# Sixteen pairs of modulation vectors of a hybrid layer, computed between the heads of the mixer instead of in the first feed-forward half

## The chip, the cores and the metric

The kernel runs on one core of a Trainium2 chip. The metric is the device time of one execution in microseconds, as the median of several runs. The engines are named as in the profile: PE is TensorE's matmuls, PEld its weight loads, DVE is VectorE, ACT is ScalarE, POOL is GpSimd, SP is the engine whose queue issues nearly all transfers of this kernel. A wait that an engine's next instruction meets stops everything behind it in that engine's queue.

## The reference

One layer of a diffusion backbone on 512 latent and 256 context tokens of 1024 features, in float32. Nine modulation vectors of 1024 features come from one matrix product on the conditioning vector (`c` for the latents, `c_ctx` for the context), and scale, shift or gate the three sub-layers:

```
mx = silu(c) @ w_ada + b_ada          # split into nine vectors, mx[0] .. mx[8]; mc the same from c_ctx
x = x + 0.5 * mx[2] * swiglu(modulate(rmsnorm(x, norm1_w), mx[0], mx[1]), ffn1_w_in, ffn1_w_out)
u = modulate(rmsnorm(x, norm2_w), mx[3], mx[4])
p = u @ w_mix_in                      # q, k, v of 8 heads, decays, gates, pooling input, branch gates
x = x + mx[5] * mixer(p)              # 8 heads of a two-way delta-rule scan, a pooling branch, output projection
x = x + 0.5 * mx[8] * swiglu(modulate(rmsnorm(x, norm3_w), mx[6], mx[7]), ffn2_w_in, ffn2_w_out)
out = rmsnorm(x, final_norm_w)
```

The context goes through the first two lines and through the mixer's q, k, v with its own vectors. Vectors 0 to 4 are needed before the mixer begins; 5 is needed only after the last head, at the mixer's output, and 6 to 8 only in the second feed-forward half.

## The kernel before

All big products take float32 operands as two parts of a shorter format, so each becomes three matmuls (`whi` by `hhi`, `whi` by `hlo`, `wlo` by `hhi`); a weight tile is loaded into a staging tile and split by a cast on ACT (`whi`, L119) and a subtraction on DVE or POOL (`wlo`, L120). The order of the instructions on each engine is made by a scheduler when the program is built, from the order of the code and its own idea of when things are ready; on the chip each engine then follows its fixed order.

The 72 feature tiles of the nine modulation vectors are computed in pairs by `ada_steps`. A pair takes two loads of 512 KB of `w_ada` into the staging tile `stg`, of which there are two and which all weights of `weights` share; 16 matmuls of a 32-column operand `sc` (L150); a copy of the sums to `ada` on DVE (L153); two transposes on PE (L157); a reduction (L159) and two additions of the bias (L162) on DVE. `ada_steps` is a generator that stops once, after the copy.

- The first sixteen tiles of vectors 0 and 1 are made ahead of the first half-step, from a staging pool of their own.
- Tiles 16 to 71, which are 28 pairs, are in the list `ada_left`. The first half-step (`ffn`) calls `trickle` four times in each group's output projection and twice in each pair of its input projection. Each call finishes the pair that is open and starts the next one, so a pair's copy lies a whole call away from its transposes. 26 pairs go this way. `LATE = 2` pairs are left, which are computed whole, by `ada`, after the half-step's call.
- The mixer then runs ten iterations of a loop over k. In one, the scan of head k (`scan`), the inverses of head k+1 (`invert`) and the norms of head k+2 (`front`) are interleaved by the string `ORDER`; then come the projections of head k+3 (`head`: weights of k, q and v, products at L132, a short convolution L583), the gate of head k+1 (`gate`) and some of the 16 branch gates (`extra`, by the table `SHARE`, which has 3 and 2 in the first two iterations, 6 and 5 in the last two and none between). The products of L132 need no scan and stand between the scan's short matmuls in PE's order. The scan's first matmul in an iteration is L973 with `vt` on its left.

The SP queue issues the loads of `stg` (L110 for weights, L146 for `w_ada`), of the decay rows `crow` (L808), and the stores of each head's result `y` (L1017) and of the branch gates (L1033), in one fixed order; a load of `stg` waits until the tile's last reader is done.

Of the kernel before, what the change touches and what calls it, by code (L numbers as in the profile page):

```python
# [41 lines left out]
def layer_kernel(ctx, tc, a, out):  # L42
# [42 lines left out]
    sc = xs.tile([128, KT, 32], F32, name="sc")  # L85
# [21 lines left out]
    def weights(src, k0, nk, c0, engs=(act, dve)):  # L107
        """128 columns of a matrix, in two float32r parts."""
# [5 lines left out]
    def halves(w, first=act, second=dve):  # L114
        """Up to four feature tiles of 128 columns, in two float32r parts."""
# [7 lines left out]
    def job(w, act_hi, act_lo, ks, parts, new=None):  # L123
        """One tile of 128 output features: w (K on the partition) times the activations."""
# [16 lines left out]
    def ada_steps(cts, tags="bb", room=None):  # L141
# [10 lines left out]
        s = xs.tile([128, 256], F32, tag="ada", name="ada", bufs=1)  # L152
# [5 lines left out]
        r = xs.tile([128, 2, 2], F32, tag="adar", name="adar", bufs=2)  # L158
# [6 lines left out]
    def mod_scale(n, k, mod, rn):  # L165
        """(1 + scale) * norm weight for feature tile k."""
        dve.tensor_scalar(out=eff[:, n, k, :], in0=mods[:, mod * 8 + k, :], scalar1=1.0,
                          scalar2=vec[:, 0, rn + k:rn + k + 1], op0=ALU.add, op1=ALU.mult)
# [5 lines left out]
    def rstd_of(ssq, n, dim):  # L174
        """ssq: [128, n] sums of squares with the token on the partition."""
# [23 lines left out]
    def rstd_rows(tmp, acc, parts, ssq=None, tag="b", dtag=("diag", 1)):  # L199
        """Root mean square, inverted, of every token, the same on all partitions."""  # L200
# [29 lines left out]
    # [C11 C12; C21 C22] = [A11 A12; A21 A22] [B11 B12; B21 B22], rows: two tiles of 128 output features,  # L230
    # columns: two halves of the tokens, inner: two halves of the 8 feature tiles
    def products(n2, more):
        """The places of the right-hand operands: B11, B21, B22, T4, T1, T2, T3, and B12."""
# [9 lines left out]
    def blocks_of(t, k, n2, dst):  # L243
        """The blocks of B themselves, of feature tile k."""
# [3 lines left out]
    def blocks(dst):  # L248
        """The operands of the products of the blocks themselves."""
        return lambda j, part, k: dst[(0, 7)[j] if k < 4 else (1, 2)[j]][part][:, k % 4]  # L250

    def combine(tmp, b11, b12, b21, b22, n2, put, bufs=1, eng=dve):
        """The other right-hand operands from the blocks; overwrites b12, and without bufs b11 and b22."""
# [19 lines left out]
    def side_by_side(ws, outs, rhs, ks):  # L273
        """Products of several weights, one feature tile k of all of them after another."""
# [7 lines left out]
    def plain(src, c0, rhs, n2, k0=0, nk=KT, tags=None):  # L282
        """As quad, by eight multiplications, from the blocks themselves."""
# [8 lines left out]
    def quad_weights(tmp, deep, src, c0, rows=None):  # L292
        """256 columns of src on their way to the seven left-hand operands, in the order of their use."""
# [3 lines left out]
        for i in range(2):  # L297
            # the inner halves: the first and the last four feature tiles, or the even and the odd ones
# [21 lines left out]
    class Quads:  # L320
        """The quads of a list of (src, c0, rows), one after another."""
# [15 lines left out]
    def quad(quads, gen, w1, w6, rhs, n2):  # L337
        """Two tiles of output features of all tokens: C11 (in PSUM), C12, C21, C22."""
# [155 lines left out]
    def last_pair(ahi, alo):  # L494
        """The last two feature tiles' share of the output, first for the latents, and the mixer's input from it."""
# [7 lines left out]
        w_first.extend(weights(a["w_mix_in"], 0, KT, c) for c in (3 * D, D))  # L503
        for k in range(KT):
            mod_scale(2, k, 4, R_N2)
# [23 lines left out]
    LATE = 2  # L529
    ada_left = [(t, t + 1) for t in range(16, 72, 2)]  # L530
# [3 lines left out]
    def trickle():  # L534
        for g in ada_open:
            next(g, None)
            if len(ada_left) == 24:
                mod_gate(1, 2, True)
# [8 lines left out]
    while ada_left:  # L547
        ada(ada_left.pop(0), "ag")
    mod_gate(3, 5, False)
# [39 lines left out]
    def head(h):  # L589
        """Project, convolve k, q and v of one head."""  # L590
# [640 lines left out]
```

## Time and profile before

| | |
|---|---|
| median of 3 runs | 1804.71 us |
| lowest and highest | 1804.62 and 1808.05 us |
| span of the profiled execution | 1807.2 us |
| PE busy | 1649.1 us (91%) |
| PEld busy | 1486.5 us (82%) |
| DVE busy | 1365.7 us (76%) |
| ACT busy | 943.9 us (52%) |
| POOL busy | 632.3 us (35%) |
| moved by DMA | 184.06 MB, 102 GB/s on the mean |

The span is that of one execution taken by the profiler; it lies inside the range of the timed runs and 2.5 us above their median. The first half-step's products run from about 84 to 600 us of it, the mixer's input from there to about 640 us, the scans of the eight heads from about 740 to 1236 us, and the rest is the mixer's output and the second half-step. Busy shares are a mean over all of these, so a stage is read by its own stretch.

### The profile page before, as it was taken

To read this page: it belongs to the slowest core of one execution; us is meant where nothing else is said; L and a number is where in the kernel's file an instruction comes from. 1 tells how busy PE (TensorE), PEld (TensorE's weight loads), DVE (VectorE), ACT (ScalarE), POOL (GpSimd) and SP (SyncE) were. 2 spreads that over 40 slices of the span, in tenths; PEclk is the share of its full clock that TensorE was granted. 3 is DMA by queue.
4 is the path that set the end of the run, shared out by engine and by line. 5 is a ranking of instruction groups with operands and counts; after the bars stand their busy time and mean duration, and the time that the engine had idled before them with its cause. 6 is when DMAs were issued, how large, how long until landed. Compare 5 with 4: busy or idle time off the path is not lost.

```text
span 1807.2 us, 34927 instructions
## 1 busy us (share of the span) xinstructions
PE 1649.1 (91%) x13432; PEld 1486.5 (82%) x13432; DVE 1365.7 (76%) x2647; ACT 943.9 (52%) x2088; POOL 632.3 (35%) x669
## 2 busy tenths in 40 slices
PE   6899999999999999899999999999987888888886
PEld 4798998989999778777877888777877888888886
DVE  5778888897878874457776778645549899899886
ACT  5533343434344465757777776564426444444454
POOL 2244434444534020332233321100005556555642
PEclk9999999999999999999999999999998999899988
DMA  9455455351212353522221212247431222222221
GB/s 272 117 147 160 133 144 156 110 161 62 76 59 71 117 169 120 130 64 60 53 59 47 67 40 66 59 132 224 129 105 48 77 88 83 82 82 85 79 82 59
DMA packets 250971, 184.06 MB, mean 102 GB/s; under 512 B 7008, under 2 KB 238133, under 8 KB 250677
## 3 DMA queue, kind: packets, MB, share of 16 engines
q1 hardware_dynamic: 250368, 181.65, 34.4%
q8 instruction: 106, 1.74, 0.4%
q14 instruction: 60, 0.49, 0.1%
q10 hardware_dynamic: 437, 0.18, 0.0%
HBM read 170.22 MB, written 11.58 MB: 101 GB/s over the span
## 4 chain that ended last, share of the span: by engine, by line
PE 55%; DVE 25%; issue 6%; ACT 5%; DMA 5%; POOL 2%; SPq 0%; POOLq 0%; ACTq 0%; DVEq 0%
PE b L132 12%; PE b L345 11%; PE g L345 7%; PE a L345 6%; DVE wlo L120 4%; DVE cv L583 2%; DVE q L474 2%; DVE alo L189 2%; PE b L279 2%; DVE t L257 2%; DVE xT L437 1%; PE a L708 1%; PE a L132 1%; PE b L150 1%; PE g L132 1%
## 5 line engine op out<-in xcount | busy, mean ns | idle before, releaser
L119 ACT CAST whi<-qst 128x512 fp32r<-128x512 f32 (+2 forms) x288 | 159.1, 554 | 164.7 <-PE b L345 66.7
L120 DVE TENSOR_TENSOR wlo<-qst,whi 128x512 fp32r<-128x512 f32 (+2 forms) x288 | 215.5, 757 | 16.7 <-ACT whi L119 16.4
L119 ACT CAST whi<-qs 128x512 fp32r<-128x512 f32 (+2 forms) x216 | 117.7, 554 | 171.4 <-POOL qs L309 82.1
L132 PE MATMUL b<-hhi,whi 128*128 128x512 f32 (+1 forms) x528 | 188.4, 386 | 0.0
L132 PE MATMUL b<-hlo,whi 128*128 128x512 f32 (+1 forms) x528 | 188.3, 385 | 0.0
L132 PE MATMUL b<-hhi,wlo 128*128 128x512 f32 (+1 forms) x528 | 187.7, 386 | 0.0
L308 POOL TENSOR_TENSOR qs<-qst 128x512 f32<-128x512 f32 (+2 forms) x72 | 92.7, 1287 | 253.1 <-DMA qst<-in_ffn_w_in_dram 70.2
L313 POOL TENSOR_TENSOR qs<-qst,qs 128x512 f32<-128x512 f32 (+2 forms) x72 | 87.4, 1214 | 198.1 <-DVE wlo L120 181.1
L119 ACT CAST whi<-stg 128x512 fp32r<-128x512 f32 x154 | 94.3, 620 | 112.7 <-PE b L132 70.4
L120 DVE TENSOR_TENSOR wlo<-qs,whi 128x512 fp32r<-128x512 f32 (+2 forms) x144 | 104.9, 728 | 49.7 <-ACT whi L119 49.4
L345 PE MATMUL b<-ehi,wlo 128*128 128x384 f32 (+1 forms) x240 | 84.3, 351 | 45.7 <-DVE wlo L120 45.7
L179 POOL TENSOR_TENSOR rs<-rs,mhalf 128x4 f32<-128x4 f32 (+2 forms) x13 | 14.0, 1077 | 294.6 <-DVE rs L177 279.0
L188 ACT CAST ahi<-q 128x384 fp32r<-128x384 f32 (+1 forms) x118 | 55.3, 473 | 118.1 <-DVE q L474 60.8
L583 DVE SCALAR_TENSOR_TENSOR cv<-raw,vec,cv 128x772 f32<-128x772 f32 (+1 forms) x96 | 100.4, 1046 | 11.6 <-ACT cv L581 8.3
L345 PE MATMUL g<-hhi,whi 128*128 128x384 f32 (+1 forms) x320 | 105.5, 330 | 2.5 <-ACT whi L119 2.5
L345 PE MATMUL g<-hhi,wlo 128*128 128x384 f32 (+1 forms) x320 | 103.6, 324 | 3.6 <-DVE wlo L120 3.6
L132 PEld LDWEIGHTS b<-hlo,whi 128*128 128x128 f32 x528 | 94.6, 191 | 14.9
L132 PEld LDWEIGHTS b<-hhi,whi 128*128 128x128 f32 x528 | 94.5, 191 | 14.9
L132 PEld LDWEIGHTS b<-hhi,wlo 128*128 128x128 f32 x528 | 94.0, 191 | 15.0
L345 PE MATMUL g<-hlo,whi 128*128 128x384 f32 (+1 forms) x320 | 103.6, 324 | 0.0
L120 POOL TENSOR_TENSOR wlo<-stg,whi 128x512 fp32r<-128x512 f32 x46 | 65.4, 1429 | 90.6 <-ACT whi L119 70.5
L312 POOL TENSOR_TENSOR qst<-qst 128x512 f32<-128x512 f32 (+2 forms) x72 | 95.6, 1327 | 0.6
(480 smaller groups left out, 5459.6 us busy)
## 6 DMA issues: line engine op xcount, KB each, us to landing
qst<-in_ffn_w_in_dram SPq DMA_DIRECT2D x80, 512.0 KB, 3.5
stg<-in_w_ada_dram SPq DMA_DIRECT2D x56, 512.0 KB, 4.6
stg<-in_w_mix_in_dram SPq DMA_DIRECT2D x49, 512.0 KB, 3.9
qst<-in_ffn_w_out_dram SPq DMA_DIRECT2D x40, 256.0 KB, 2.7
adx<-in_w_ada_dram SPq DMA_DIRECT2D x16, 512.0 KB, 7.1
qst<-in_ffn_w_out_dram SPq DMA_DIRECT2D x16, 512.0 KB, 3.8
crow<-cumd SPq DMA_DIRECT2D x16, 384.0 KB, 8.8
stg<-in_ffn_w_in_dram SPq DMA_DIRECT2D x8, 512.0 KB
```

The lines of the kernel that those rows point to most:

```text
L119: (first.copy if first is act else first.tensor_copy)(out=hi[:, :n], in_=w)
L120: second.tensor_tensor(out=lo[:, :n], in0=w, in1=hi[:, :n], op=ALU.subtract)
L132: pe.matmul(res[p][:, :m], lhsT=ww(i), rhs=hh(k)[:, o:o + m], start=(i == 0 and j == 0), stop=(i == n - 1 and j == 2))
L188: act.copy(out=hi, in_=src)
L189: dve.tensor_tensor(out=lo, in0=src, in1=hi, op=ALU.subtract)
L257: eng.tensor_tensor(out=t, in0=x, in1=y, op=ALU.subtract)
L279: pe.matmul(x, lhsT=ww(k), rhs=rhs(j, part, k), start=n + e == 0, stop=n + e == len(ks) + 1)
L308: pool.tensor_tensor(out=s1, in0=a21, in1=a22, op=ALU.add)
L312: pool.tensor_tensor(out=a21, in0=a11, in1=a21, op=ALU.subtract)
L313: pool.tensor_tensor(out=s2, in0=a12, in1=s2, op=ALU.subtract)
L345: pe.matmul(o, lhsT=ww[:, k], rhs=rhs(j, part, k), start=first and k + i == 0, stop=k + i == nh + 1, skip_group_check=not first)
L583: dve.scalar_tensor_tensor(out=cv[:, :n], in0=raw[:, t:t + n], scalar=tap[t], in1=cv[:, :n], op0=ALU.mult, op1=ALU.add)
```

## The change

`ada_left` keeps only tiles 16 to 39 (12 pairs: vectors 2, 3 and 4), and `LATE` is 0, so that all of them go through `trickle`. The other 16 pairs (vectors 5 to 8) are in a new list `ada_late`. The mixer's loop takes from it by the table `ADA_SHARE`, after the branch gates of an iteration: two pairs in each of the iterations k = 0 and 1, three in each of k = 2 to 5. There `ada` runs a pair whole, without the stop between the copy and the transposes. The tiles `sc`, `ada` and `adar` move to pools that live longer, and the gate of vector 5 (`mod_gate(3, 5, False)`) follows the loop. Apart from that, comments are gone.

```diff
-    sc = xs.tile([128, KT, 32], F32, name="sc")
+    sc = base.tile([128, KT, 32], F32, name="sc")
...
-        s = xs.tile([128, 256], F32, tag="ada", name="ada", bufs=1)
+        s = wp.tile([128, 256], F32, tag="ada", name="ada", bufs=1)
...
-        r = xs.tile([128, 2, 2], F32, tag="adar", name="adar", bufs=2)
+        r = wp.tile([128, 2, 2], F32, tag="adar", name="adar", bufs=2)
...
         w_first.extend(weights(a["w_mix_in"], 0, KT, c) for c in (3 * D, D))
+        while ada_left or ada_open:
+            trickle()
         for k in range(KT):
...
-    LATE = 2
-    ada_left = [(t, t + 1) for t in range(16, 72, 2)]
+    LATE = 0
+    ada_left = [(t, t + 1) for t in range(16, 40, 2)]
+    ada_late = [(t, t + 1) for t in range(40, 72, 2)]
...
-            if len(ada_left) == 24:
+            if len(ada_left) == len(range(24, 40, 2)):
                 mod_gate(1, 2, True)
...
-    while ada_left:
-        ada(ada_left.pop(0), "ag")
-    mod_gate(3, 5, False)
     fp_cm.__exit__(None, None, None)
...
     SHARE = (3, 2, 0, 0, 0, 0, 0, 0, 6, 5)
+    ADA_SHARE = (0, 0, 2, 2, 3, 3, 3, 3, 0, 0)
...
         for f in extra[:SHARE[k + 2]]:
             f()
+        for cts in ada_late[:ADA_SHARE[k + 2]]:
+            ada(cts)
+        ada_late = ada_late[ADA_SHARE[k + 2]:]
         extra = extra[SHARE[k + 2]:]
-    assert not extra
+    assert not extra and not ada_late
+    mod_gate(3, 5, False)
```

What it does to the order on the engines shows at three places.

On PE, in an output projection of the first half-step (`ahi`, `alo` are the two parts of its right operand), one pair goes; the rows with a minus stood there before:

```order
 L345 MATMUL b<-alo,whi 128x384
 L345 MATMUL b<-ahi,wlo 128x384
-L157 MATMUL b<-ident,ada 128x128 x2
-L150 MATMUL b<-stg,sc 32x128 x16
 L345 MATMUL g<-ahi,whi 128x384
 L345 MATMUL g<-alo,whi 128x384
```

The transposes of one pair and the matmuls of the next stood between two products; now the products follow each other.

On PE, at the start of a head's scan in the mixer, before (`vt`, `kf`, `qf` are the head's v, k and q, `S` the scan's state, `hhi` and `hlo` the input of the projections):

```order
L973 MATMUL g<-vt,L 128x128 x2
L764 MATMUL a<-ident,kf 128x128 x6
L985 MATMUL g<-vw,kt 128x128 x2
L771 MATMUL a<-ident,qf 128x128 x4
L824 MATMUL a<-kf 128x128 x4
L952 MATMUL g<-S,kf 128x128 x2
L132 MATMUL b<-hhi,whi 128x512
L132 MATMUL b<-hhi,whi 128x256
L132 MATMUL b<-hlo,whi 128x512
```

And after the change, further into such a start, from the transposes of the second of three pairs to the first product of the next head's weights; the first pair's matmuls stand ahead of `L973 g<-vt,L`, its transposes between the six of `L764`, and the second pair's matmuls before these rows:

```order
L824 MATMUL a<-kf 128x128 x2
L157 MATMUL b<-ident,ada 128x128 x2
L150 MATMUL b<-stg,sc 32x128 x8
L797 MATMUL a<-ident,vf 128x128 x4
L150 MATMUL b<-stg,sc 32x128 x8
L797 MATMUL a<-ident,vf 128x128 x2
L157 MATMUL b<-ident,ada 128x128 x2
L833 MATMUL a<-qf,kf 128x128 x4
L985 MATMUL g<-vw,kt 128x128 x2
L132 MATMUL b<-hhi,whi 128x512
L132 MATMUL b<-hhi,whi 128x256
L132 MATMUL b<-hlo,whi 128x512
```

Before, the products of L132 begin ahead of the second of the scan's steps; now the first of them stands behind the second `L985`, and all three pairs stand ahead of it.

On the SP queue, around the store of one head's result, before:

```order
L1017 DMA yg_dram<-y 128x512
L110 DMA stg<-in_w_mix_in_dram 128x8x128 x2
L808 DMA crow<-cumd 128x6x128
L110 DMA stg<-in_w_mix_in_dram 128x8x128
L808 DMA crow<-cumd 128x6x128
L110 DMA stg<-in_w_mix_in_dram 128x8x128
```

And after:

```order
L808 DMA crow<-cumd 128x6x128 x2
L146 DMA stg<-in_w_ada_dram 128x8x128
L1017 DMA yg_dram<-y 128x512
L146 DMA stg<-in_w_ada_dram 128x8x128 x5
L110 DMA stg<-in_w_mix_in_dram 128x8x128 x4
```

Six loads of `w_ada` now stand around the store, and the four weight loads of the next head and gate behind all of them.

## Rows read from the trace of the kernel before

**Rows 1.** Windows: span, busy us (x) of PE PEld DVE ACT POOL, PEclk, DMA, GB/s

```profile
84.00:600.00 516.00, 498.28 (x3468) 476.78 (x3467) 431.95 (x849) 212.85 (x446) 221.16 (x197) 1.00 0.40 116
798.00:1188.00 390.00, 371.41 (x4538) 312.08 (x4537) 284.32 (x686) 280.33 (x737) 102.48 (x182) 1.00 0.22 57
```

**Rows 2.** Windows, between the fourth output projections of the first half-step's successive groups

```profile
171.00:274.04 103.04, 100.18 (x778) 95.83 (x777) 86.54 (x183) 40.76 (x86) 45.34 (x40) 1.00 0.50 144
274.04:375.94 101.90, 99.60 (x776) 95.58 (x775) 86.40 (x176) 40.75 (x86) 45.60 (x40) 1.00 0.50 145
375.94:472.36 96.42, 93.02 (x578) 90.06 (x577) 83.32 (x154) 40.23 (x86) 45.08 (x40) 1.00 0.29 88
472.36:567.33 94.97, 90.88 (x506) 89.24 (x505) 76.82 (x144) 40.74 (x86) 44.73 (x40) 0.98 0.22 67
```

**Rows 3.** The same windows, DVE's copy L153 alone (one for each pair)

```profile
171.00:274.04 103.04, 3.29 (x8) 1.00 0.50 144
274.04:375.94 101.90, 3.28 (x8) 1.00 0.50 145
375.94:472.36 96.42, 0.81 (x2) 1.00 0.29 88
```

**Rows 4.** Timeline of PE around one pair: start, us, engine, line, instruction

```profile
247.80 0.38 PE L157 MATMUL b<-ident,ada 128*128 128x128 f32 x2
248.11 1.08 PE L150 MATMUL b<-stg,sc 128*32 128x128 f32 x32
249.12 0.44 PE L345 MATMUL g<-ahi,whi 128*128 128x384 f32 x1
```

**Rows 5.** Timeline of PE, the two late pairs between the half-step and the mixer

```profile
618.42 1.08 PE L150 MATMUL a<-stg,sc 128*32 128x128 f32 x32
...
626.44 0.64 PE L150 MATMUL a<-stg,sc 128*32 128x128 f32 x16
...
631.75 0.38 PE L157 MATMUL g<-ident,ada 128*128 128x128 f32 x2
```

**Rows 6.** Windows: iterations k = 0 to 5 together, k = 1, and k = 5

```profile
798.10:1138.40 340.30, 322.94 (x3924) 272.23 (x3923) 251.03 (x596) 251.23 (x670) 97.61 (x173) 1.00 0.22 55
...
855.10:914.10 59.00, 55.10 (x665) 46.52 (x664) 42.26 (x100) 42.84 (x114) 16.95 (x33) 1.00 0.18 47
1088.30:1138.40 50.10, 47.63 (x604) 39.56 (x603) 34.96 (x95) 36.71 (x102) 8.21 (x15) 1.00 0.22 61
```

**Rows 7.** Timeline of PE in iteration k = 1: its first and second L985

```profile
858.38 0.71 PE L985 MATMUL g<-vw,kt 128*128 128x128 f32 x4 [1.77 <-DVE vw L976]
...
868.03 0.61 PE L985 MATMUL g<-vw,kt 128*128 128x128 f32 x4
```

**Rows 8.** Windows: from the first matmul of k = 1 to behind that second L985

```profile
855.10:868.40 13.30, 11.53 (x86) 10.28 (x84) 9.01 (x24) 8.68 (x32) 5.94 (x12) 1.00 0.16 43
```

**Rows 9.** Windows: products L132 alone (PE, PEld), the same stretch and k = 5

```profile
855.10:868.40 13.30, 6.76 (x30) 4.29 (x29) 1.00 0.16 43
...
1088.30:1138.40 50.10, 28.30 (x95) 16.57 (x94) 1.00 0.22 61
```

**Rows 10.** DMA issues, 84 to 600 us and 798 to 1138 us: KB, median us to landing

```profile
stg<-in_w_ada_dram SPq DMA_DIRECT2D x52, 512.0 KB, 4.7
...
stg<-in_w_mix_in_dram SPq DMA_DIRECT2D x24, 512.0 KB, 3.9
```

**Rows 11.** Lines, 798 to 1138 us: the two halves of a weight's split

```profile
L120 POOL TENSOR_TENSOR wlo<-stg,whi 128x512 fp32r<-128x512 f32 x27 | 39.4, 1467 | 57.7 <-ACT whi L119 38.7 <-PE b L132 14.3 <-PE g L973 3.7
L119 ACT CAST whi<-stg 128x512 fp32r<-128x512 f32 x48 | 29.2, 618 | 33.6 <-PE b L132 27.0 <-issue 3.6 <-POOL L L840 2.8
```

**Rows 12.** Windows of 4 us around a fall of PE's clock

```profile
496.00:500.00 4.00, 1.80 (x11) 1.48 (x10) 4.00 (x10) 3.18 (x7) 0.00 (x0) 1.00 0.01 2
500.00:504.00 4.00, 4.00 (x16) 4.00 (x16) 3.40 (x7) 1.14 (x2) 1.10 (x1) 0.57 0.50 158
504.00:508.00 4.00, 4.00 (x25) 4.00 (x24) 1.40 (x2) 1.63 (x3) 3.29 (x4) 1.00 0.32 108
```

## The prediction

> **What bounds the kernel now.** I read the busy time of the two stages first [rows 1]. In the first half-step PE is busy for 498.28 of 516 us, in the iterations of the mixer's loop for 371.41 of 390. PE is thus the engine whose order sets the time in both, and work that is moved from one to the other is taken off one full queue and put on another. What can differ is only what such work costs in each place: how much of it fills time that PE would wait anyhow, and what waits it brings.
>
> **What the first half-step gives back.** 14 of the 26 pairs go. The output projections of successive groups are a clean ruler [rows 2]: the same products lie between the fourth projections, with eight pairs in the first two stretches, two in the third and none in the last [rows 3], where a window with no copy has no row. They take 103.04, 101.90, 96.42 and 94.97 us, so a pair costs (103.04 - 94.97)/8 = 1.01, (101.90 - 94.97)/8 = 0.87 and (96.42 - 94.97)/2 = 0.73 us. The pairs that go are the last four of the first stretch, all eight of the second, both of the third: 4.0 + 6.9 + 1.5 = 12.4 us. This is a floor, since the last stretch holds a slowdown of its own: from 500 to 504 us PE ran at 0.57 of full clock and did 16 matmuls where the next 4 us have 25 [rows 12], some 1.4 us lost. Against 93.5 instead of 94.97 the sum is 4 x 1.19 + 8.4 + 2.9 = 16.1. The ceiling is PE's whole time for a pair, transposes and matmuls from 247.80 to 249.12, 1.32 us [rows 4], so 18.5. I take 14. The copy on DVE, 3.29/8 = 0.41 us [rows 3], and the loads go too, but PE is the engine waited for, so they are in that difference.
>
> The two late pairs stood between the half-step and the mixer. Their matmuls and last transposes take 1.08 + 0.64 + 0.38 = 2.1 us [rows 5] in a chain of short steps; the rest of their work lies in waits of the context's norm. I take 2.5 with the small DVE steps, between 1.5 and 3.5. Given back: **16.5 us**, between 14 and 22.
>
> **What the mixer pays: work.** 16 pairs of 1.32 us are 21.1 us of PE. If all of this lay in waits, it would cost nothing; over iterations k = 0 to 5 PE waits for only 340.30 - 322.94 = 17.4 us in all [rows 6], in pieces like the 1.77 us at an `L985` [rows 7]. So the work is mostly paid in full.
>
> **What the mixer pays: waits.** The order shows where a batch goes: to the start of the next head's scan, one pair ahead of its first matmul and the others between its first steps, and on the SP queue ahead of the four weight loads of the next head. Before, the products L132 stand between these steps and fill their waits. With only two `stg` tiles, each load now has to wait until PE has read the one before it, so I followed a batch of three from its first matmul (time 0), with 3.9 us from issue to landing, the value of this stage; in the busier first stage it was 4.7 [rows 10].
> - Pair 1 is loaded in time. PE reads its first tile by 0.5, the second by 1.0; this lets the loads of pair 2 go, which land at about 4.7 and 5.2.
> - By then PE has done the first steps of the scan (whose first `L985` waits for DVE, now as before [rows 7]) and of `front`. Pair 2 is read from 4.7 to 6.8, between them.
> - Pair 3: issued at 5.5 and 7.1, landed at 9.5 and 11.1. PE comes to it at about 8 and waits 1.5 and 0.6 us.
> - The next head's first weights get a free tile when pair 3's first is read, at 10.0: landed at 14.2, cast at 14.9 (0.62), subtracted on POOL by 16.3 (1.47) [rows 11]. The first four products can run ahead of that.
>
> So until about 16 us PE has three pairs, four products (0.7) and the other matmuls up to the second `L985`. In iteration k = 1 before, this second `L985` comes at 868.03, and of the 13.3 us to behind it PE is busy for 11.53, L132 takes 6.76 of them [rows 8, 9]; what is left, 4.8, is a floor for the others, and by their start-to-start slots on the timeline I make it 5.8, since the products' tails overlap them. PE then waits 16 - 4.0 - 5.8 - 0.7 = 5.5 us, where it waited 1.77 before [rows 7]: 3.7 more. With a batch of two the weights' tile is free at 5.2, so the products begin at 10.1 and run freely at 11.4: 11.4 - 2.7 - 5.8 - 0.7 = 2.2, or 0.4 more than before. Behind that point the products, later but all still to be done, keep PE full, and the iteration is longer by the work and by the new wait.
>
> Batches of two start k = 1 and 2 (0.4 each), of three k = 3, 4 and 5 (3.7 each). The last batch stands inside k = 5, which has the products of one gate only; before, 95 products ran there [rows 9], pulled ahead from later, and now they run later, so I add 2 us of waiting there. New waits: 0.8 + 11.1 + 2.0 = 13.9. The bounds: nothing (no row of before has these loads in this stage), and 25, with 4.7 us for a load, three in a row, and the floor of 4.8 above. The few DVE steps of a pair, 0.9 us, stand on an engine that is busy for 284 of 390 us [rows 1], and cost only as part of the copy for which the transposes wait; nothing stands between the two now.
>
> **The sum.** 21.1 + 13.9 - 16.5 = +18.5 us. Against the profiled execution that is 1807.2 + 18.5 = 1825.7; its span is 2.5 us above the median of the runs, so I forecast **1823.2 us**, 1.0% slower.
>
> **The rivals.**
>
> *A, the forecast* (+18.5): chance 0.44. For it speaks that the new order puts all three pairs, and no product, in the steps of the scan that wait most.
>
> *B, the clock falls as well.* PE's clock fell to its lower level of 1.2 GHz for most of 500 to 504 us, behind a window in which PE was busy for 1.80 of 4 us; one fall cost about 1.4 us [rows 12]. The new starts have waits of 1 to 2 us close together among short matmuls. Five such starts with one fall each are 7 us more: +25.5, 1830. Against it: the wait of 1.77 us at 856 us went by with the clock at 1.00 in its window [rows 8], and no window of the loop's six iterations shows less [rows 6]. Chance 0.22. The Trainium skill (TensorE: Matmul & The Clock Gate, section Why this matters for your kernels) warns that gaps on PE between bursts bring the lower rate back; the fall at 500 us agrees in kind, and no run here yet shows it in these iterations.
>
> *C, the waits don't come.* If loads and copies are ready when PE comes to them, only work is left: 21.1, less what falls into waits that are there anyhow, between 0 and 8, less 16.5: +4.6 to -3.4, about 1806. What must hold is that a pair's loads land before PE reaches it; the 3.9 us speak against it, and that the scheduler put the pairs apart speaks a little for it. Chance 0.21.
>
> *D, faster.* PE's waits in the loop take the work. PE's weight loads are busy for only 312.08 of 390 us in the loop, but for 476.78 of 516 in the first half-step [rows 1]: by this reading 78 us are free in the one and 39 in the other. If the 17.4 us of waits [rows 6] took all but 3.7 of the 21.1, the time would be 3.7 - 16.5 = -12.8, 1792. The point from which it decides: a pair must cost less than 16.5/16 = 1.03 us in the loop, against 1.01 in the first half-step at the most favourable reading of the same rows and 1.32 bare. Against it: those waits are latencies at `L985`, `L952` and the like, and PE follows its order, in which the pairs don't stand at them. Chance 0.13. The Trainium skill (Perfetto Trace Analysis, Identifying the Most-Contended Engine) states that matmul busy time is no good measure of PE's headroom and names weight-load busy time instead; this is that reading, and by it the mixer is the better place for the pairs.
>
> That the change doesn't move the work can't be: the order shows all 14 + 2 pairs gone there and come here.
>
> **How the numbers follow.** 0.2% (3.6 us) is about what a measurement of this kernel can tell from no change. A and B are slower; C is the same for most of its width (0.15), else slower by a little (0.05) or faster (0.01); D is faster. Faster 0.14, same 0.15, slower 0.71. The range reaches from the lower part of C to the upper bound of the waits with the loss of B in part, 21.1 + 25 - 16.5 + 5 = +35: 1801 to 1840. A's own range is 1811 to 1833 (14 to 22 given back, 7 to 21 of new waits).
>
> **What would show it.** In the half-step, the stretches between the fourth projections all near 94 to 95 us, and the mixer beginning some 16 us sooner. In the loop, iterations k = 1 and 2 of about 60 to 62 us and k = 3 and 4 of about 65 to 67 us, against the (340.30 - 50.10)/5 = 58 of k = 0 to 4 before [rows 6]; PE's waits named after `stg<-in_w_ada_dram`, after DVE's copy L153 and, at the first product, after the split of the weights; few or no products in the first 10 to 15 us of an iteration. PE's clock below 1.00 in these would be B. I am wrong if a pair costs about 1 us there (C, D), that is, if these iterations grow by no more than 3 to 4 us each; or if the half-step gives back much less than 14, for instance because another wait (a load of `qst`, a split) steps in where the pairs stood.

## The result, and the profile after

The changed kernel takes 1862.84 us (1861.19 to 1865.53, four runs), the kernel before, in four runs, 1806.38 us: ratio 1.0306, 95% interval 1.0283 to 1.0329, 56 us slower. I forecast 1823.2 us, 18.5 slower, and a range of 1801 to 1840. The direction was right, the size was not: the time lies 23 us above the range.

The page of the changed kernel, busy time and the granted clock in 40 slices (the clock is below full speed in more of the slices of the middle than before):

```profile
PE 1681.7 (90%) x13432; PEld 1507.3 (81%) x13432; DVE 1375.1 (74%) x2647; ACT 942.2 (51%) x2086; POOL 622.7 (33%) x669
...
PEclk9999999999999899999999999899998899899888
```

Windows of the changed kernel between the fourth output projections of successive groups, answering to [rows 2]: span, busy us (x) of PE, PEld, DVE, ACT, POOL, then PEclk, DMA, GB/s.

```profile
170.41:271.96 101.55, 97.93 (x644) 94.40 (x643) 85.56 (x170) 40.79 (x86) 44.48 (x40) 0.97 0.34 104
271.96:367.88 95.92, 91.83 (x506) 89.39 (x505) 79.90 (x143) 40.23 (x86) 44.14 (x40) 0.98 0.21 67
...
463.71:559.55 95.84, 91.78 (x506) 89.36 (x505) 79.90 (x143) 40.23 (x86) 44.07 (x40) 0.98 0.21 67
```

Four pairs are left in the first stretch, none in the other three. Those take 95.8 to 95.9 us, not 94 to 95: PEclk is 0.98 in each of them, where it was 1.00 in all but the last before. The four together give back 7.2 us (396.33 - 389.14), and the first scan begins at 790.90 instead of 798.10 (not at about 740, as the section on the profile before has it): **7 us given back, not 16.5**, in this execution.

The seven iterations from k = 0 to k = 6, each from the scan's first matmul to the next one's; first the changed kernel, then two of the kernel before with its sum over all seven:

```profile
790.90:848.97 58.07, 56.05 (x697) 46.98 (x695) 41.41 (x100) 41.57 (x111) 14.53 (x29) 1.00 0.22 51
848.97:912.94 63.97, 60.50 (x736) 50.52 (x732) 43.83 (x107) 43.13 (x114) 16.88 (x30) 0.97 0.32 84
912.94:978.50 65.56, 61.03 (x736) 50.72 (x732) 47.24 (x110) 43.73 (x115) 17.50 (x36) 0.97 0.30 82
978.50:1048.91 70.41, 64.00 (x770) 52.66 (x766) 46.10 (x112) 43.09 (x115) 16.92 (x33) 0.95 0.35 91
1048.91:1119.57 70.66, 62.55 (x770) 51.19 (x766) 48.50 (x116) 43.37 (x115) 16.76 (x30) 0.98 0.30 85
1119.57:1174.28 54.71, 46.24 (x710) 36.50 (x707) 35.96 (x117) 34.29 (x97) 8.12 (x15) 0.89 0.46 131
1174.28:1245.20 70.92, 68.06 (x683) 55.81 (x682) 38.45 (x98) 32.97 (x76) 4.75 (x10) 0.94 0.29 83
```

```profile
971.77:1030.73 58.96, 54.92 (x666) 46.43 (x665) 42.48 (x100) 42.86 (x115) 17.23 (x33) 1.00 0.18 47
...
1138.40:1188.21 49.81, 48.57 (x616) 39.96 (x615) 33.28 (x90) 29.11 (x69) 4.87 (x10) 1.00 0.24 70
sum 390.11, PE 371.52 PEld 312.19 DVE 284.32 ACT 280.34 POOL 102.48; mean PE 53.07 PEld 44.60 DVE 40.62 ACT 40.05 POOL 14.64
```

454.30 instead of 390.11 us: **64.2 us more, where I forecast 35**. k = 1 to 4 grow by 4.9, 8.0, 11.5 and 13.1 us, k = 5 and 6 together by 25.7. The clock was full in every one of these windows before and is below it in six of seven now.

Where the time goes inside an iteration is seen in k = 3. First the products L132 alone in its first 16 us, before and after (PE, PEld, PEclk, DMA, GB/s):

```profile
971.77:987.77 16.00, 8.61 (x38) 5.75 (x38) 1.00 0.14 39
```

```profile
978.50:994.50 16.00, 0.94 (x4) 0.61 (x4) 0.89 0.70 198
```

38 products became 4. What holds them up stands on the SP queue: the next head's weights (L110), issued from 968.90 before, 2.9 us ahead of the iteration, now follow four loads of `w_ada` (L146) and begin 8.6 us into it. Timeline of SP, before and after:

```profile
968.90 5.39 SPq L110 DMA_DIRECT2D stg<-in_w_mix_in_dram  x2
```

```profile
978.20 6.87 SPq L146 DMA_DIRECT2D stg<-in_w_ada_dram  x4
987.09 12.99 SPq L110 DMA_DIRECT2D stg<-in_w_mix_in_dram  x4
```

PE's order, made by the scheduler, has the products as late: the first one, at 992.80 us, shows no wait for its weights. PE's timeline in the same iteration: two waits for loads of the third pair, the second `L985`, the first product, and a wait that I had not foreseen.

```profile
986.39 0.65 PE L150 MATMUL b<-stg,sc 128*32 128x128 f32 x16 [0.66 <-DMA stg<-in_w_ada_dram]
...
988.61 1.07 PE L150 MATMUL b<-stg,sc 128*32 128x128 f32 x16 [0.92 <-DMA stg<-in_w_ada_dram]
...
992.43 0.61 PE L985 MATMUL g<-vw,kt 128*128 128x128 f32 x4
992.80 0.60 PE L132 MATMUL b<-hhi,whi 128*128 128x512 f32 x2
...
1001.04 0.49 PE L997 MATMUL g<-vn,aqk 128*128 128x128 f32 x2 [2.94 <-ACT vn L980]
```

What that last wait comes from is read in the waits of 978.5 to 1002 us, on all engines (total, times, longest):

```profile
POOL wlo L120 <- ACT whi L119: 4.5, 1, 4.5
DVE tm L866 <- POOL ti L856: 3.9, 1, 3.9
PE g L997 <- ACT vn L980: 2.9, 1, 2.9
...
ACT vn L980 <- DVE vw L976: 1.9, 1, 1.9
```

POOL stands at the split of the late weights; behind it in its queue are three more splits and the clearing of `ti` (L856); DVE waits for that with the step of the inverses, and behind that step stands `vw` (L976) of the scan, for which ACT waits, and PE for ACT. A load that is late for the products thus stops the scan through three queues. Over all seven iterations, PE's waits for the pairs' loads and at `L997`, after, and at `L997` before (total, times, longest):

```profile
PE b L150 <- DMA stg<-in_w_ada_dram: 8.7, 9, 2.1
PE g L997 <- ACT vn L980: 5.5, 2, 2.9
```

```profile
PE g L997 <- ACT vn L980: 1.4, 2, 0.7
```

The stop at `L997` comes in k = 3 and 4 alone and is worth some 4 us of the 64.

### The profile page after: what moved, and what is told of

Read it like the earlier page. It is cut to its first block, busy times and chain, and to the rows that moved or that the text cites. A ratio compares the mean times of both kernels' runs of the same rounds, so it can differ in the third digit from the quotient of the medians.

```text
span 1862.3 us, 34917 instructions
## 1 busy us (share of the span) xinstructions
PE 1681.7 (90%) x13432; PEld 1507.3 (81%) x13432; DVE 1375.1 (74%) x2647; ACT 942.2 (51%) x2086; POOL 622.7 (33%) x669
## 5 line engine op out<-in xcount | busy, mean ns | idle before, releaser
L120 DVE TENSOR_TENSOR wlo<-qst,whi 128x512 fp32r<-128x512 f32 (+2 forms) x288 | 219.9, 774 | 15.7 <-ACT whi L119 15.6
L132 PE MATMUL b<-hhi,whi 128*128 128x512 f32 (+1 forms) x528 | 186.7, 386 | 6.4 <-ACT whi L119 6.4
L132 PE MATMUL b<-hlo,whi 128*128 128x512 f32 (+1 forms) x528 | 188.8, 386 | 0.0
L132 PE MATMUL b<-hhi,wlo 128*128 128x512 f32 (+1 forms) x528 | 186.6, 386 | 0.9 <-POOL wlo L120 0.9
L132 PEld LDWEIGHTS b<-hhi,whi 128*128 128x128 f32 x528 | 94.8, 194 | 22.5 <-ACT whi L119 7.0
L583 DVE SCALAR_TENSOR_TENSOR cv<-raw,vec,cv 128x772 f32<-128x772 f32 (+1 forms) x96 | 92.7, 965 | 22.5 <-ACT cv L581 16.5
L132 PEld LDWEIGHTS b<-hlo,whi 128*128 128x128 f32 x528 | 95.6, 193 | 15.8 <-issue 0.2
L132 PEld LDWEIGHTS b<-hhi,wlo 128*128 128x128 f32 x528 | 94.3, 192 | 17.3 <-POOL wlo L120 1.5
L120 DVE TENSOR_TENSOR wlo<-stg,whi 128x512 fp32r<-128x512 f32 x108 | 73.9, 689 | 42.2 <-ACT whi L119 39.7
```

The costliest lines, as they stand in the source:

```text
L120: second.tensor_tensor(out=lo[:, :n], in0=w, in1=hi[:, :n], op=ALU.subtract)
L132: pe.matmul(res[p][:, :m], lhsT=ww(i), rhs=hh(k)[:, o:o + m], start=(i == 0 and j == 0), stop=(i == n - 1 and j == 2))
L583: dve.scalar_tensor_tensor(out=cv[:, :n], in0=raw[:, t:t + n], scalar=tap[t], in1=cv[:, :n], op0=ALU.mult, op1=ALU.add)
```

## The experiments

Medians of each kernel, and the ratio to runs of the kernel before on the same chip:

| kernel | us | ratio | 95% interval |
|---|---|---|---|
| e1_no_late | 1796.44 | 0.9921 | 0.9901 to 0.9940 |
| e2_no_load | 1839.28 | 1.0162 | 1.0146 to 1.0178 |
| e3_load_only | 1855.91 | 1.0252 | 1.0233 to 1.0271 |
| e15_act_reads | 1824.41 | 1.0077 | 1.0055 to 1.0098 |
| e16_act_reads_work | 1841.63 | 1.0172 | 1.0153 to 1.0192 |
| e4_own_tile | 1897.96 | 1.0494 | 1.0462 to 1.0526 |
| e10_two_each | 1866.28 | 1.0334 | 1.0310 to 1.0358 |
| e14_one_by_one | 1876.93 | 1.0391 | 1.0356 to 1.0426 |
| e12_last_scans | 1892.46 | 1.0471 | 1.0446 to 1.0496 |
| e18_none_in_k5 | 1872.62 | 1.0338 | 1.0324 to 1.0353 |
| e8_none_late | 1814.42 | 1.0031 | 1.0019 to 1.0042 |
| e19_late4 | 1823.90 | 1.0071 | 1.0055 to 1.0086 |
| e20_late8 | 1842.09 | 1.0173 | 1.0158 to 1.0188 |
| e21_late16 | 1873.01 | 1.0349 | 1.0327 to 1.0371 |
| e17_second_half | 1821.82 | 1.0064 | 1.0047 to 1.0080 |

**What the first stage gives back, alone** (e1_no_late):

```diff
-        for cts in ada_late[:ADA_SHARE[k + 2]]:
-            ada(cts)
```

> The changed kernel with its 16 late pairs left out altogether (vectors 5 to 8 are set to zero, so this part of the computation is missing); PE's order in the loop is again that of the kernel before. It measures alone what the first half-step gives back. My forecast said 16.5 us, so 1790 us. The changed kernel's trace says about 7 (its loop begins 7 us sooner, and each stretch without pairs holds a clock fall of 3.4 us), so 1799 us with the loop back at about 390 us from k = 0 to k = 7 and no clock fall in it. If the loop stays long, its cause is not the pairs but the tiles that moved to other pools.

By the ratio, 14.3 us faster than before (10.9 to 17.9; by the medians 12.1): near my 16.5, and not the 7 of the changed kernel's trace. The loop is back at 391.3 us (779.1 to 1170.37). The profiled execution is the fastest of the six, 1788.01 us, and its first scan begins 19 us sooner than before. In its windows the first three are stretches of the first half-step, with four pairs and twice with none, the last is k = 1:

```profile
170.26:268.02 97.76, 95.34 (x644) 92.27 (x643) 85.68 (x170) 40.69 (x86) 45.16 (x40) 1.00 0.36 108
268.02:362.32 94.30, 89.90 (x506) 88.10 (x505) 78.70 (x143) 40.32 (x86) 44.09 (x40) 1.00 0.21 68
362.32:456.90 94.58, 91.08 (x504) 89.45 (x504) 78.08 (x143) 40.76 (x86) 43.88 (x40) 0.98 0.21 67
...
836.10:896.41 60.31, 56.46 (x665) 47.98 (x664) 42.32 (x100) 42.88 (x114) 16.97 (x34) 0.97 0.18 45
```

A stretch without pairs takes 94.30 us here at a clock of 1.00 (95.20 in e2), and at 0.98 it takes 94.58 here and 95.92 in the changed kernel. So what one fall of the clock costs in this stage doesn't stand clear of the differences between executions. The clock falls in some stretches and executions and not in others, with eight pairs too (104.94 us at 0.98 in e8's first); this kernel's runs spread from 1788.0 to 1799.9 us. In the mixer the price is clearer: k = 1, in the same order of instructions as before, takes 60.31 us with 0.97 instead of 59.03 with 1.00: 1.28 us for 2 x 0.03 x 60.31 = 3.6 us at the lower level, **0.36 us for each us at 1.2 GHz**. The k = 3 of e8, in the order of before too, takes 60.39 us at 0.97 instead of 58.96: 0.4.

**Work, loads, and the hold of the tiles.** Four kernels take the changed kernel apart: work without loads (e2), loads read by one step of PE's matmuls, with a small copy on DVE for each pair (e3), loads read by ACT when they land (e15), and those with the work (e16).

```diff
 # e2: the late pairs only
-  pe.matmul(..., lhsT=sc[:, k, :], rhs=stg[:, k, :], ...)      # stg loaded from w_ada
+  pe.matmul(..., lhsT=sc[:, k, :], rhs=ident, ...)             # no load
 # e3
+  pe.matmul(b[0:32, e * 128:(e + 1) * 128], lhsT=sc[:, 0, :], rhs=stg[:, 0, :])
 # e15, and e16 (into a tile of its own) with the work of e2 behind it
+  act.copy(out=mods[:, c, :], in_=stg[:, 0, 0:2])
```

> The late pairs multiply the resident identity instead of loaded weights: matmuls, copy, transposes and sums stay, the 32 loads and their use of the two stg tiles go (vectors 5 to 8 are wrong values). Theory L (the loads take the two tiles and the place in SP's queue ahead of the next head's weights, products come late, and the scan's steps stand without cover): the loop grows by the work alone and the copy's waits, 21 to 33 us instead of 64, so 1820 to 1832 us, few clock falls. Theory W (PE's work for the pairs and the waits of its own chain, copy and transposes, make the loss): stays above 1845 us.

> The late pairs load their weights as in the changed kernel, but only one of a load's eight pairs of matmul steps reads it, and the transposes and sums are left out (vectors 5 to 8 are not computed). Almost no PE work is left (about 2 us). Theory L: the products stay displaced, the loop grows by 64 less about 33 of slots that belong to the pairs themselves, some 25 to 35 us, so 1824 to 1834 us, with clock falls at the scans' starts. Theory W: about 1799 to 1804 us.

Both theories fall as they were put. The work without loads costs 1839.28 - 1796.44 = 43 us, more than theory L allowed; the loads with hardly any work cost 59.5 us, far more than either allowed, and only 7 less than loads and work together. The costs don't add; that work and waits for loads fill the same holes would explain it, and isn't shown. Two windows of e2, k = 1 and k = 3, have the clock at 1.00:

```profile
846.73:909.04 62.31, 58.61 (x736) 48.67 (x732) 42.77 (x106) 42.55 (x113) 17.24 (x33) 1.00 0.22 52
...
971.53:1035.71 64.18, 59.85 (x770) 50.44 (x766) 48.67 (x114) 43.91 (x116) 17.10 (x33) 1.00 0.20 51
```

PE is idle in them for 3.7 and 4.3 us, about as before (3.9 and 4.0). It is busy for 58.61 and 59.85 us where it was 55.10 [rows 6] and 54.92: 1.8 and 1.6 us more for each pair, where the forecast had 1.32.

> The late pairs' 32 loads in the same two tiles and at the same place in SP's queue, but each is read by a copy of two columns on ACT as soon as it lands, not by PE; matmuls, copy, transposes and sums of the pairs are left out (vectors 5 to 8 are not computed). Beside the run that had loads and one step of matmuls for each (1856 us) only the reader differs. Theory H (hold: a pair's tile is free only when PE, in its order, has come to it, and the loads behind it in SP's queue wait for that): 1797 to 1812 us. Theory D (the 16 MB themselves, by their time on the queue and the memory): 1840 us or more.

> The same loads read by ACT on landing, and besides them the pairs' work on PE and DVE from the resident identity (vectors 5 to 8 get wrong values): all that the changed kernel has but the hold of the tiles. The run with the work and no loads took 1839 us. Theory H: 1839 to 1848 us, 15 to 24 less than the changed kernel. Theory D: 1858 to 1866 us.

With the same loads in the same two tiles, but ACT as their reader, e15 is 31.5 us faster than e3; e16 is 21 faster than the changed kernel and only 2.4 slower than e2. So the 16 MB themselves cost little, and **what the loads cost beside the work comes with PE as their reader**: a pair's tile is free only when PE, in its order, has come to it, and the loads behind it on SP wait for that. SP's waits of this kind in the changed kernel's loop (total, times, longest):

```profile
SPq L146 <- PE b L150: 64.2, 16, 10.5
```

Not only the reader differs, though, since the scheduler made PE's order anew for each kernel. In k = 3, some 55 matmuls that belong to no pair stand between the scan's first and the first product in the changed kernel and in e3, some 30 in e2 and e16, and 10 in e15, as in the kernel before. These runs therefore don't separate what a held tile costs on the chip from the order that was built around it; e12, below, shows the first by itself.

e15 is still 28 us above e1, more than theory H said. A part of this comes with its reader again, which waits for the loads to land (total, times, longest):

```profile
ACT mods L1059 <- DMA stg<-in_w_ada_dram: 24.5, 14, 4.0
```

In k = 0, where PE's order is that of before, PE waits 3.2 us at an `L985` for a copy on ACT that stands behind such a wait. Windows of its k = 2, 3, 5 and 6:

```profile
909.30:966.89 57.59, 55.09 (x665) 46.67 (x664) 44.35 (x102) 42.22 (x117) 16.02 (x31) 1.00 0.40 110
966.89:1025.81 58.92, 56.48 (x665) 47.92 (x664) 38.85 (x102) 43.84 (x120) 16.94 (x33) 0.97 0.39 99
...
1086.81:1142.09 55.28, 44.94 (x557) 36.09 (x556) 33.75 (x94) 37.69 (x108) 8.12 (x15) 0.85 0.40 111
1142.09:1209.88 67.79, 65.36 (x662) 52.83 (x661) 36.00 (x94) 31.29 (x72) 4.74 (x10) 0.90 0.26 71
```

k = 2 and 3 take 57.6 and 58.9 us as before, though 110 and 99 GB/s pass instead of 64 and 47: the transfers cost nothing there. k = 0, 1 and 4 are 2 to 4 us longer than before. k = 5 and 6 take 123.1 instead of 99.9 us, 23 of the 32 by which the loop is longer: PE's order holds 47 products in k = 5 where it held 94, and the clock is at 0.85.

**The tile or the queue** (e4), and **the batches** (e10, e14):

```diff
-            ada(cts)
+            ada(cts, room=(mp, "adl", 1))                          # e4; its ada lies in the buffer of bgate
-    ADA_SHARE = (0, 0, 2, 2, 3, 3, 3, 3, 0, 0)
+    ADA_SHARE = (2, 2, 2, 2, 2, 2, 2, 2, 0, 0)                     # e10
                 conv_silu(weights(w_mix, 0, KT, c0 + 128 * h, EH), ...)
+            if h >= 2 and ada_late:
+                ada(ada_late.pop(0))                               # e14
```

> The changed kernel with a weight tile of its own for the late pairs (one, 4 KB per partition, in the mixer's pool), so that the two stg tiles serve the head's weights alone; the loads keep their place in SP's queue. Theory T (two shared tiles): the next head's weights no longer wait for a pair's tile, the loop costs the work and little more, 1820 to 1830 us. Theory Q (the place in SP's queue: a pair's next load waits there until PE has read the one before, and the weights stand behind it): no gain, 1850 us or more, since with one tile SP waits longer at each load.

> The changed kernel with its 16 late pairs spread two for each of the iterations k = -2 to 5, none in threes. The forecast's step (0.4 us of new waits for a batch of two, 3.7 for one of three) gives 1796 + 21.1 + 8 x 0.4 = 1820 us. If a batch of two costs what k = 1 and k = 2 grew by in the changed kernel, 4.9 and 8.0 us with a clock fall each, 1796 + 8 x 6.5 = 1848 us.

> The late pairs stand one behind each product of a head's projections (k, q, v), so that no two pairs' loads follow each other in SP's queue; in PE's order the products now stand in blocks of 48 to 70 at the start of an iteration and of the scan's 26 first steps fewer have products between them. If several loads in a row are what costs, 1820 to 1830 us. If it is the scan's steps that lose their cover, whatever the loads, 1840 us or more.

With a tile of its own the pair costs more, 101 us for 16: the SP queue stops at the pair's second load and the head's weights stand behind it, so that the first product comes 18.4 and 31.7 us into k = 1 and 3 (9.5 and 14.3 in the changed kernel). That the pair's copy `ada` shares a buffer with the branch gates here may be a part of it; no run separates this. Neither pairs in twos nor one at a time between products are cheaper, 70 and 80 us. What was wrong with my batches was not their number.

**Behind products, after the scans** (e12):

```diff
         for f in extra[:SHARE[k + 2]]:
             f()
+            for cts in ada_late[:(2 if len(ada_late) > 6 else 1) if k > 5 else 0]:
+                ada(ada_late.pop(0))
```

> The late pairs stand one or two behind each of the last eleven branch gates' products, in iterations k = 5 to 7, most of them in the block of products after the last scan; k = 0 to 4 are PE's order of the kernel before. Where products lie on both sides of a pair and no scan step waits for cover, a pair should cost its work alone: 1796 + 21.1 = 1817 us, and 1817 to 1826 us with the few that stand in the scans of k = 6 and 7. If a pair costs 4.1 us anywhere in the mixer (66 us for 16), it is 1862 us again.

This failed by the most, and shows the hold by itself on the chip, since no scan runs here. One period of its timeline on PE, 24 products and one pair:

```profile
1263.35 0.80 PE L132 MATMUL b<-hhi,whi 128*128 128x512 f32 x1 [3.52 <-ACT whi L119]
...
1271.05 0.40 PE L132 MATMUL b<-hhi,wlo 128*128 128x512 f32 x1
1271.37 1.08 PE L150 MATMUL b<-stg,sc 128*32 128x128 f32 x32
1273.00 0.44 PE L157 MATMUL b<-ident,ada 128*128 128x128 f32 x2 [0.55 <-DVE ada L153]
1277.08 0.80 PE L132 MATMUL b<-hhi,whi 128*128 128x512 f32 x1 [3.64 <-ACT whi L119]
```

SP and ACT at the same time, and two windows of the products:

```profile
1272.08 0.37 SPq L110 DMA_DIRECT2D stg<-in_w_mix_in_dram  x1
...
1276.41 1.14 ACT L119 CAST whi<-stg 128x512 fp32r<-128x512 f32 x2 [4.30 <-DMA stg<-in_w_mix_in_dram]
...
1263.35:1266.35 3.00, 3.00 (x7) 2.38 (x8) 1.28 (x2) 0.47 (x1) 0.00 (x0) 0.50 0.48 137
...
1269.35:1271.37 2.02, 2.02 (x9) 1.33 (x8) 0.00 (x0) 0.00 (x0) 0.00 (x0) 1.00 0.00 0
```

The next weights' load goes out at 1272.08, just after PE has read the pair's first tile, lands 4.3 us later, and PE waits 3.64 us at the first product. Behind the wait the clock is at 0.50, and the products follow each other by 3.00/7 = 0.43 us instead of 0.235, their pace at full clock in the rows left out. (2.02/9 is less, since the nine include one that began before the window.) A pair's 1.3 us of work so takes 13.73 - 24 x 0.235 = 8 us.

**Is k = 5 a loss of its own?** (e18)

```diff
-    ADA_SHARE = (0, 0, 2, 2, 3, 3, 3, 3, 0, 0)
+    ADA_SHARE = (0, 3, 3, 3, 3, 4, 0, 0, 0, 0)
```

> The changed kernel with its 16 late pairs in batches of three at the starts of k = 0 to 3 and of four at k = 4, so that k = 5, which has few products of its own, holds none. If the misplaced products of k = 5 (26 instead of 94, the rest behind in k = 6) are a loss of their own, k = 5 and 6 take 100 us together again, 26 less than in the changed kernel; and the four batches of three should cost 11 to 13 us each as in its k = 3 and 4, so 1796 + 4 x 12 + 16 = 1860 us. If three pairs at a scan's start cost only my forecast's 7.7 (work 4.0, waits 3.7), 1796 + 5 x 8 = 1836 us.

Windows of its k = 3, 5 and 6:

```profile
1004.39:1076.41 72.02, 65.09 (x770) 53.45 (x766) 49.10 (x118) 43.46 (x115) 16.95 (x33) 0.93 0.32 89
1150.71:1202.51 51.80, 50.04 (x610) 40.76 (x609) 37.37 (x97) 38.55 (x107) 8.19 (x15) 1.00 0.20 54
1202.51:1252.97 50.46, 47.74 (x596) 39.06 (x595) 32.44 (x89) 28.21 (x66) 4.74 (x10) 0.97 0.24 68
```

k = 5 and 6 take 102.3 us together again, but each batch of three at a scan's start costs 13 us, and the kernel is not faster, nor as fast as the 1860 us expected. So the loss is not that of k = 5: a pair costs some 4.1 us in the changed kernel (66.4/16), 4.4 and 4.8 in e10 and e18, 5.0 in e14 and 6.0 in e12.

**Other places** (e8, e19 to e21 with 0, 4, 8 and 16 pairs between the half-step and the mixer; e17 with four in the second half-step and none there):

```diff
-    LATE = 2
+    LATE = 0                    # e8, which also finishes the open pair; 4 in e19, 8 in e20, 16 in e21
 # e17: ada_left keeps tiles 16 to 63; ahead of the second half-step's call of ffn
+        ada_left.extend((t, t + 1) for t in range(64, 72, 2))
```

> The kernel before with its two boundary pairs taken into the first half-step too (all 28 pairs there, none between the half-step and the mixer). My forecast's term for the boundary was 2.5 us given back, against two pairs more at 0.5 to 0.9 each in the half-step: 1805 us, 1 us faster. By the changed kernel's trace, where the boundary gave nothing back (231.35 us against 230.76), it is 1 to 2 us slower, 1808 us; if two pairs in the last stretches also take away its clock fall, 0 to 2 us faster.

> The kernel before with four pairs instead of two between the half-step and the mixer, two fewer in the first half-step. Taking the boundary's two pairs into the half-step cost 6 us, and leaving all 16 out gave the boundary stretch 0.4 us. If pairs are nearly free at the boundary: 2 to 6 us faster than the kernel before. If each costs 1.3 or more there, as by my forecast: no change or up to 2 us slower.

> As the run before, with eight pairs at the boundary and 20 in the first half-step. If the boundary's waits take eight pairs (16 loads of 512 KB are about 40 us of loading by 4 to 5 us for two): 4 to 8 us faster than the kernel before; if only the first two to four fit, slower than with four pairs.

> The same 16 pairs that the changed kernel moves, all at the boundary between the half-step and the mixer (12 in the first half-step). If a pair there costs its loads one behind another, 4 to 5 us, 1796 + 16 x 4.5 = 1868 us, no better than in the loop; if the boundary's waits (20 us of PE) take most of it, 1800 to 1815 us.

> The kernel before with the last four pairs (the gate of the second feed-forward half, two of them from the boundary and two from the first half-step) among the products of the second half-step, where no other weights use the stg tiles and PE waits for 81 of 498 us. If a pair costs there what it costs in the first half-step, no change: 1806 to 1811 us. If its waits take the work, 2 to 5 us faster than the kernel before; if it holds a queue up as in the mixer, 10 us slower or more.

The stretch from the last group's projection to the first scan with two pairs (before), four and sixteen, one window of each kernel:

```profile
567.34:798.10 230.76, 211.18 (x1520) 177.92 (x1519) 144.26 (x281) 130.21 (x261) 48.58 (x87) 0.96 0.41 119
```

```profile
571.05:815.00 243.95, 220.96 (x1588) 184.46 (x1587) 142.35 (x289) 130.55 (x261) 49.76 (x87) 0.92 0.44 121
```

```profile
558.59:865.30 306.71, 251.83 (x1996) 201.06 (x1995) 153.94 (x338) 130.71 (x261) 49.76 (x87) 0.86 0.50 137
```

With none it takes 230.40 us in e8, 231.35 in the changed kernel and 227.56 in e1. The first two pairs thus cost between nothing and 3 us, which single executions don't tell apart; the next cost (306.71 - 230.76)/14 = 5.4 us each. The two pairs should stay where they were: taken into the first half-step they make the kernel 6 us slower (e8), 5 of it in the half-step's four stretches (401.24 us instead of 396.33). Four pairs in the second half-step bring nothing either (12 us slower); its own stretch grows by 3 to 5 us, and the rest, in earlier stages whose clock differs from run to run, I have not settled. No placement tried beats the kernel before.

## Why the prediction was wrong in size

In the profiled executions 55.1 us were lost (1862.3 - 1807.2) against 18.5 forecast. Of the 36.6 us between them the loop has 64.2 - 35 = 29.2, the stages around it the rest, 7.4.

By the seven windows of each kernel, PE's idle time in the loop grew by 17.3 us (454.30 - 418.43 of busy time, against 390.11 - 371.52) and its busy time by 46.9. The forecast had 13.9 for the first and 21.1 for the second. **By this reading the waits were nearly right, and two terms of busy time failed: the clock, which the sum put at nothing, and the work, which it put at 1.32 us for a pair.** As an estimate, work of 26 to 29, idle time of 17.3 and a clock loss of 14 to 17 make 57 to 63 of the 64.2.

- **What is given back: 16.5 us forecast, 14.3 measured by e1's runs.** The changed kernel's profiled execution shows 9 of it (64.2 - 55.1): its four stretches take 389.14 us, those of e1, the same instructions, 381.28 (170.26 to 551.54), and those of e15, again the same, 384.50 (171.20 to 555.70). This is a difference between executions. The clock may be a part of it, but e15's stretches have PEclk at 0.98 as well, and e1's stretch at 0.98 is as short as its others. I had read the fall of [rows 12] as the accident of one stretch and subtracted it; falls are common in stretches without pairs, and come in some with them.
- **The boundary's 2.5 us:** the stretch without its two pairs takes 231.35 us in the changed kernel, 230.40 in e8 and 227.56 in e1, against 230.76. That is nothing to 3 us, so this term is neither confirmed nor refuted.
- **The mixer's work, 21.1 us, was too low.** At 1.6 to 1.8 us of busy PE for a pair, as in k = 3 and 1 of e2, it is 26 to 29, an estimate. With nothing but this work, e2's loop takes 427.2 us (788.7 to 1215.96), 37 more than before: much like my sum, by another way. Of these, 8 us are idle PE (26.6 instead of 18.6).
- **The new waits, 13.9 us with 25 as the bound:** PE's idle time grew by 17.3. In k = 1 to 4 it grew by -0.4, 2.1, 2.4 and 5.7 us and in k = 5 and 6 together by 7.6, where I had 0.4, 0.4, 3.7, 3.7 and 5.7. The profile's busy time also holds matmuls that last longer because nothing overlaps them, so this is the lesser reading of the waits.
- **The steps of a batch: right up to the first product.** In k = 3 the third pair waits 0.66 and 0.92 us where I had 1.5 and 0.6, and the first product begins 14.3 us into the iteration, where I had 14.9, the end of the cast. Behind it a smaller step failed, "Behind that point the products, later but all still to be done, keep PE full". The scan itself was stopped behind the late weights in the queues of POOL, DVE and ACT, and waited 2.94 us at `L997`; in the whole loop that wait grew by some 4 us. I had named what the late weights do to PE, and not what stands behind their split on the engines that make it.
- **The clock, rival B, was to be in the sum.** By the windows PE was at the lower level for 2 x (0.03 x 63.97 + 0.03 x 65.56 + 0.05 x 70.41 + 0.02 x 70.66 + 0.11 x 54.71 + 0.06 x 70.92) = 38 us in the loop. At 0.36 us for each (k = 1 of e1) to 0.45 (the products of e12, (0.43 - 0.235)/0.43) that is 14 to 17 us, an estimate; B had 7. It may be less, since k = 3 of e15 shows no cost of a fall (58.92 us at 0.97, against 58.96). The 1.00 that I held against B was that of the kernel before. Four microseconds of k = 1, in which PE came to the late weights and the clock fell:

```profile
856.00:860.00 4.00, 1.67 (x9) 1.41 (x8) 2.39 (x11) 1.70 (x4) 3.23 (x3) 0.87 0.54 151
```

  The Trainium skill (TensorE: Matmul & The Clock Gate, Why this matters for your kernels) warns of gaps on PE between bursts. The trace agrees in this window, where PE is busy for 1.67 of 4 us; the falls of the half-step and of e1's k = 1 come without late loads of pairs.
- **C and D fell.** D's condition was a pair below 1.03 us in the loop; it costs 4.1. PEld's 78 free us [rows 1] were no room, since PE was not waiting for weight loads but kept from its next step. The Trainium skill (Perfetto Trace Analysis, Identifying the Most-Contended Engine) judges PE's headroom by MFU, the arithmetic done as a share of the peak, and by weight-load busy time. By the second of these, D's reading, the mixer is the better place; here it was not, and the measurement decides.

That it is not the 16 MB is shown by e16 against e2 and by e15 against e3; that PE as the reader holds the tile and the queue, by SP's waits and by e12. Open is how much of the loop's loss the hold makes on the chip, and how much the order of PE that the scheduler built around it: in the iterations with a scan no run has the one without the other.

## What to carry to other kernels

The cost of moved work is not its busy time alone but also what it holds: a load that PE itself reads keeps its tile, and the queue behind it, until PE comes to it in order. A load that another engine reads on landing holds them for less, at the price of waits in that engine's queue. In the first half-step, where the big weights have tiles of their own (`qst`), the same pairs cost 1 us (that this is the reason was argued, not tried), so look first at who shares the tile and who is next on the queue. Then follow a late load through every queue that touches it, not only to the engine that wants it, and put the clock's price into the sum wherever new waits appear among short matmuls. Where a scheduler orders the engines, an experiment changes more than its edit: compare the orders before saying that only one thing differs.

## What the runs showed of the hardware

- Whether the clock falls in a stretch of the same instructions differs from execution to execution. A stretch of the half-step without pairs took 94.30 to 95.20 us at 1.00 (e1, e2) and 94.58 to 95.92 at 0.98 (e1, the changed kernel); with eight pairs it took 101.90 to 103.15 at 1.00 ([rows 2], e8) and 104.94 at 0.98 (e8). The runs of e1 spread over 12 us, with the granted clock of a whole execution between 0.956 and 0.964.
- A fall to 1.2 GHz cost 0.36 to 0.4 us for each us of it among the scan's short matmuls (k = 1 of e1, k = 3 of e8) and 0.45 among dense products (e12); in k = 3 of e15 no cost shows.
- With tiles read on landing, 110 GB/s passed in k = 2 instead of 64 at no cost (57.59 and 57.61 us): the memory and the queue had that room.
